# Where the tiles of the normed input begin in SBUF: one place modulo 256 bytes instead of four, with three staging buffers

## The chip, the cores and the metric

The kernel runs on one core of a Trainium2 chip. The time is device microseconds (us) from start to end of one launch. The kernel before took 1615.73 us as the median of three runs (1615.65 to 1615.97).

## What is computed

A trunk of two layers works on 272 tokens (16 learned ones and 256 of the input) of 1024 features, in float32. The first layer computes all 272 tokens; the second needs its outputs for the last 256 alone. Cut to what matters here:

```python
def hybrid_layer(h_res, ...):
    h = rmsnorm(h_res, n_mix_pre)
    proj = jnp.einsum('bld,de->ble', h, w_in)          # 1024 x 17424
    (a_b, a_c, a_x, s_z, s_xbc, s_dt, r_q, r_k, r_v, r_g,
     sb_q, sb_k, sb_v, gate_logits) = jnp.split(proj, IN_SPLITS, axis=-1)
    ...                                                # four token mixers: y_a, y_b, y_c, y_d
    up = jnp.einsum('blnw,nwd->blnd', branches, w_branch)
    merged = jnp.sum(sigmoid(gate_logits) * up, axis=2)
    h_res = h_res + rmsnorm(merged @ w_out, n_mix_post)
    f = rmsnorm(h_res, n_ffn_pre) @ w_ffn_in           # 1024 x 5632
    f = (silu(f_gate) * f_up) @ w_ffn_out              # 2816 x 1024
    return h_res + rmsnorm(f, n_ffn_post)
```

## The kernel before, in words

Features lie on the 128 partitions and tokens on the free axis. The normed input of a sublayer is eight tiles of 128 features (k = 0 to 7). A product is to have float32's precision, so each operand is kept as two addends in float32r: the input tile as `x1` and `x2`, the weight tile as `w1` and `w2`, and every product of a weight tile with an input tile takes three matmuls: (w1, x1), (w2, x1), (w1, x2). The loop is in `mm` (lines 305 to 314, the matmul itself on L313). The weight is the stationary operand (128 columns, 512 bytes of a partition), the input the moving one (256 to 272 columns). While a matmul streams its input, the weight of the next matmul is loaded; the trace shows the loads as a row of their own, PEld. Three matmuls of one k tile are called a triple below.

A job is one tile of 128 output features: eight triples, 24 matmuls into one PSUM bank, and then an evacuation by VectorE. The first layer has 136 such projections of the normed input before the mixers and 44 in the feed-forward part, all 272 columns wide: 180 jobs, 4320 matmuls. The second layer has 116 jobs of 256 columns (2784 matmuls), 44 of 272 (1056), 16 of 258 (384) and 4 of 260 (96). The other matmuls of L313 (2976) have tiles named `hold` as the moving operand: outputs of mixers, of the merge and of the feed-forward part.

`run_jobs` emits the jobs; the order on TensorE is as emitted. The first three jobs after a norm (one in the first norm of all) run side by side, k tile by k tile, so that nine matmuls in a row read one k tile.

Weights come in the order of use (`weights`, line 280): SyncE issues a DMA of 512 KB into a staging buffer `raw` (L287), ScalarE rounds it to `w1` (L298), VectorE subtracts to `w2` (L301). `raw` has four buffers, `w1` and `w2` five each (NW). A staging buffer is free again when L301 has read it. One weight per layer is 16 columns wide (`narrow`, line 316); its staging buffer is read by L328 into `wdt`. A scheduler puts the instructions of ScalarE and VectorE in order; weights have a high priority in it.

The two addends of the input are made in `prenorm` (line 432), by ScalarE (L452) and VectorE (L457), in tiles of 272 floats, eight buffers for each addend. In the second layer a norm starts where the layer needs it, but a matmul may read all 272 columns, or 256 from column 16 on.

Where a tile lies in a partition: the weight tiles take 4096 bytes each and begin, all of them, at 192 modulo 256 in the partition, and so does each k slice of 512 bytes. The tiles of `x1` and `x2` take 272 x 4 = 1088 bytes, which is 4 x 256 + 64, one behind the other. The start of each is therefore 64 bytes further modulo 256 than that of its neighbour: eight tiles fall on four places, two on each. `x1` and `x2` of one k have the same place. Below, the place of a read is the number of bytes modulo 256 from a weight tile's start to the first byte of the input that the matmul reads: 0, 64, 128 or 192.

Of the kernel before, what the change touches and what calls it, by code (L numbers as in the profile page):

```python
# [15 lines left out]
P = 128  # L16
D = 1024
KT = 8
# [8 lines left out]
LATE, LATER = 2, 2  # L27
PS = {"mm": 4, "sc": 1, "ty": 3}
# [9 lines left out]
# token tiles of the sequence mixers and where their columns lie side by side  # L38
# [4 lines left out]
# branches in the order they are merged: index into w_branch  # L43
# [3 lines left out]
# the activation tables that have a function, the one that is loaded by default first  # L47
# [5 lines left out]
def plan():  # L53
    """Weight tiles in the order the kernel uses them: (key, first k tile, k tiles)."""
    out = []

    def proj(l, col):
        out.append((("in", l, col), 0, KT))

    for l in range(DEPTH):  # L60
        def gu(n, m0=0, m1=KT):
            for m in range(m0, m1):
                proj(l, GATE + n * D + m * P)
                out.append((("br", l, n, m), 0, KT))

        def conv(m0, m1):
            for m in range(m0, m1):
                for base in (A_C, A_X, A_B):
                    proj(l, base + m * P)

        for h in range(8):
            for base in (B_K, B_Q, B_V):
                proj(l, base + h * P)
        conv(0, 2)
        proj(l, S_DT)
        for g in range(4):
            for col in (S_XBC + D + g * P, S_XBC + D + 512 + g * P,
                        S_XBC + 2 * g * P, S_XBC + (2 * g + 1) * P,
                        S_Z + 2 * g * P, S_Z + (2 * g + 1) * P):
                proj(l, col)  # L80
            gu(BR_SB, 2 * g, 2 * g + 2)
        for g in range(4):
            for base in (R_K, R_Q, R_V, R_G):
                proj(l, base + 2 * g * P)
                proj(l, base + (2 * g + 1) * P)
        conv(2, 5)
        gu(BR_SSD)
        conv(5, 8)
        gu(BR_RET)
        gu(BR_CONV)  # L90
        for m in range(KT):
            out.append((("out", l, m), 0, KT))
        for j in range(FT):
            out.append((("fi", l, j), 0, KT))
            out.append((("fi", l, FT + j), 0, KT))
        for m in range(KT):
            out.append((("fo", l, m), 0, 8))
            out.append((("fo", l, m), 8, 7))
            out.append((("fo", l, m), 15, 7))
    return out  # L100


def width(key):
    """Columns of a weight tile"""
    return 16 if key[0] == "in" and key[2] == S_DT else P


# per-layer columns of the packed vectors
V_NPRE, V_NPOST, V_FPRE, V_FPOST = 0, 8, 16, 24
V_CA = 32           # 3 x 8  # L110
V_CW = 56           # 4 x 16
V_CB = 120          # 16
V_SN = 136          # 8
V_SD = 144          # 8
V_AL = 152          # 16, the same on every partition
V_DB = 168          # 1, heads on partitions
V_N = 169

# columns of the constants
# [12 lines left out]
def constants():  # L132
    c = np.zeros((P, C_N), np.float32)
    s = np.arange(P)[:, None]
    u = (np.arange(T)[None, :] >= s).astype(np.float32)
    for i, (t0, _) in enumerate(STILE):
        c[:, C_MASK + OFF[i]:C_MASK + OFF[i] + T - t0] = u[:, :T - t0]
    c[:, C_UP:C_UP + T] = u
    c[:, C_MASK:C_MASK + WID] *= 0.25
    rel = np.arange(T)[None, :] - s  # L140
    for h in range(4):
        lg = np.log(1.0 - 2.0 ** (-5.0 - h))
        c[:, C_DEC + h * T:C_DEC + (h + 1) * T] = np.where(
            rel >= 0, np.exp(lg * np.maximum(rel, 0)), 0.0) * (256 ** -0.5)
    inv = (np.float32(10000.0) ** (-np.arange(P, dtype=np.float32) / np.float32(P))).astype(np.float32)
    pos = (PADROWS + np.arange(T)).astype(np.float32)
    ang = (inv[:, None] * pos[None, :]).astype(np.float32).astype(np.float64)
    c[:, C_COS:C_COS + T] = np.cos(ang)
    c[:, C_SIN:C_SIN + T] = np.sin(ang)
    c[:, C_ID:C_ID + P] = np.eye(P)  # L150
    c[:, C_ONE:C_ONE + P] = 1.0
    # lhsT[s, s'] = -1 where s >= s'
    c[:, C_NTRI:C_NTRI + P] = -np.tril(np.ones((P, P)))
    c[:, C_NONE:C_NONE + P] = -1.0
    import ml_dtypes
    b = np.zeros((P, 2 * P), np.float32)
    b[:, :P] = np.eye(P)
    b[:, P:] = np.where(s >= np.arange(P)[None, :], -1e30, 0.0)
    return c, b.astype(ml_dtypes.bfloat16)
# [54 lines left out]
class Trunk:  # L214
    """Features on partitions, tokens on the free axis, throughout.

    The tensor engine takes its work in the order it is emitted here: one tile of 128 output
    features after the other, with the stages of the sequence mixers (generators) between them.
    """
# [16 lines left out]
    # ---- tiles  # L236
# [18 lines left out]
    def table(self, ins):  # L255
        """Functions that need a table keep their order on the scalar engine."""
        if self.last_table is not None:
            self.order(ins, self.last_table)
        self.last_table = ins

    def order(self, ins, before):
        """ins after `before` on the engine of both"""
        self.tc.add_manual_dep(
            ins.ins, before.ins.name,
            mybir.DependencyInfo(mybir.DependencyClass.NoSync, mybir.DependencyReason.DATA),
            reason="order")
# [11 lines left out]
    # ---- weights  # L278
    def weights(self, key):
# [5 lines left out]
        with self.tc.high_priority(offset=1000000):  # L285
            raw = self.t("raw", [P, KT * P], 4)
# [7 lines left out]
            # the first ones in parts, for products to start early  # L294
# [10 lines left out]
    def mm(self, ps, w, k, x1, x2, c0, nk, passes=(0, 1, 2)):  # L305
        """One tile of 128 features against one tile of outputs, in three exact passes."""
# [9 lines left out]
    def narrow(self, ps, key):  # L316
        """Sixteen features, in float32: even and odd k tiles in two halves of the array's columns."""
# [4 lines left out]
        with self.tc.high_priority(offset=1000000):  # L322
            raw = self.t("raw", [P, KT * P], 4)
            nc.sync.dma_start(
                raw[:, :n], self.a["w"][self.woff:self.woff + P * n].rearrange("(p f) -> p f", p=P))
# [10 lines left out]
    def keep_warm(self, n):  # L336
        """Products that nothing reads: the array's clock halves when it idles for a few microseconds."""
# [9 lines left out]
    def run_jobs(self, jobs, first=0, late=0):  # L347
        """jobs: (key, first column, k tiles, operands, evacuation). The `first` jobs run side by
        side, so that each tile of operands is used as soon as it is there. Their outputs, and
        those of `late` more, leave PSUM once the norm's sum is there."""  # L350
# [44 lines left out]
    def two(self, src, c0, scale=1.0):  # L395
        """src (in SBUF or PSUM) as two addends that float32r holds exactly."""
# [10 lines left out]
    def parts(self, src):  # L407
        """src as two addends that float32r holds exactly"""
# [5 lines left out]
    def total(self, out, parts):  # L414
        """Sum over the partitions"""
# [15 lines left out]
    # ---- norms  # L431
    def prenorm(self, c0, vcol, ready=None):
        """The two addends of h * weight; the root mean square is applied where products leave PSUM.
        `ready`: brings a tile of h up to date."""
# [5 lines left out]
        def operands(k):  # L440
            """h's tile k as two addends, and the one after it brought up to date"""
            w = self.v(vcol + k)
            x1 = self.t("x1", [P, T], KT, F32R)
            x2 = self.t("x2", [P, T], KT, F32R)
# [21 lines left out]
            if k == KT - 1 and ready is not None:  # L466
                # prepared before this norm: the tiles that there is room for
# [52 lines left out]
    def postnorm(self, c0):  # L520
        """Gives what norms a tile of the sublayer, and what adds it to h."""
# [17 lines left out]
    # ---- mixers  # L539
    def softplus_part(self, z, tmp, bias=None):  # L540
        """tmp <- ln(1 + exp(-|z + bias|)); the caller adds max(z + bias, 0)."""
# [60 lines left out]
    def silu2(self, out, v):  # L602
        """out <- 2 silu(v), v in SBUF"""
# [4 lines left out]
    def conv4(self, ps, ct, out, cs=0):  # L608
        """Four taps and twice the SiLU of one tile of xbc."""
# [11 lines left out]
    def scaled_silu(self, ps, out):  # L621
        """out <- 2 silu(ps * rstd)"""
# [8 lines left out]
    def ssd_jobs(self, g):  # L631
        """B, C, xs and z of a group; all but z come doubled, z too."""
# [31 lines left out]
    def regions(self):  # L664
        """(index, first token, tokens, first column, where the columns start)"""
# [5 lines left out]
    def both(sc, col, n, step=T):  # L671
        """n columns at col, and n more a step further"""
# [3 lines left out]
    def to_tok(self, srcs):  # L676
        """Transposed token tiles: two full ones in one bank, the last one in another."""
# [20 lines left out]
    def ssd_mix(self):  # L698
        """All groups, one stage after the other."""
# [3 lines left out]
        for g in range(4):  # L703
# [3 lines left out]
            # C B^T under the causal mask; both are doubled, and the mask has a quarter  # L707
# [7 lines left out]
            # xs * dt, tokens on partitions  # L715
# [54 lines left out]
    def ssd_finish(self, out):  # L770
        nc, c0 = self.nc, self.c0
        rr = slice(c0, T)
        # the outputs are doubled by the doubled gate: so is their root mean square
# [126 lines left out]
    def ret_mix(self, h, u):  # L900
# [13 lines left out]
        # values less their mean over the head's width: the outputs then have mean zero  # L914
# [129 lines left out]
    def layer(self, l):  # L1044
# [11 lines left out]
        def late(gen, after=()):  # L1056
            """A generator that starts when others are done"""
# [38 lines left out]
    def run(self, depth):  # L1096
# [19 lines left out]
        # what is loaded after this many tiles of weights  # L1116
# [47 lines left out]
```

## Time and profile before

| | |
|---|---|
| median of three runs | 1615.73 us (1615.65 to 1615.97) |
| the profiled execution, first to last instruction (span) | 1614.1 us |
| median less that span | 1.6 us |
| PE busy | 1599.6 us, 99% of the span |
| matmuls of L313 with the normed input | 8640, 1108.5 us |
| matmuls of L313 with `hold` | 2976, 374.3 us |
| mean granted clock of TensorE | 0.996 |

PE is TensorE's matmuls, PEld its weight loads, DVE is VectorE, ACT ScalarE, POOL GpSimd, SP SyncE; L313 is a line of the kernel. The profile gives the profiled execution by its span alone. Matmuls overlap in their records: one is listed with some 290 ns, but they start every 119 to 126 ns, so the pace is read from starts, or from stretches cut at starts. A row of the windows view gives a stretch (begin and end in us from the span's start), its length, the busy time of PE in it and how many matmuls touch it (those that began before or end behind it too), the granted clock as a share of 2.4 GHz, and the share and rate of the DMA. Its last line sums the stretches. Where the stretches are the triples of one place, each begins at the start of the first matmul of a triple and ends at the start of the next triple.

### The profile page before, as it was taken

Reading aid. Unit: us, or ns where it says so; the run is one execution under the profiler, and the core shown is the slowest. Engines: PE = TensorE matmul, PEld = TensorE weight load, DVE = VectorE, ACT = ScalarE, POOL = GpSimd, SP = SyncE. Lnnn points to the kernel's source line nnn. Section 1 sums busy time; section 2 is a strip of 40 time slices with the busy share of each in tenths; the row PEclk is TensorE's granted clock in tenths of the full one; section 3 lists DMA queues with packets and bytes.
Section 4 is the critical chain, followed back from the end, with each engine's and each line's share of the span. In section 5 each row is a group of like instructions: output and inputs, shape, how many; then the busy total and the mean of one; then the engine's idle time right before and its main releaser. Section 6 shows DMA issues by size and latency. Waiting matters only on the chain.

```text
span 1614.1 us, 31341 instructions
## 1 busy us (share of the span) xinstructions
PE 1599.6 (99%) x12732; PEld 1562.3 (97%) x12732; DVE 1104.0 (68%) x1821; ACT 776.1 (48%) x1142; POOL 301.2 (19%) x284
## 2 busy tenths in 40 slices
PE   9999999999999999999999999999999999999997
PEld 8999999999999999999999999999999999999997
DVE  7557788977866556665465578889878666576643
ACT  5544444445533456444464444444455444564442
POOL 3000003541311112221110000035414111212210
PEclk9999999999999999999999999999999999999999
DMA  7435554434455554555544446544445555545552
GB/s 256 140 120 172 176 178 158 145 118 144 160 179 171 176 177 136 185 176 162 178 141 145 134 146 199 182 171 144 132 144 178 183 188 183 184 158 184 184 181 78
DMA packets 74015, 264.26 MB, mean 164 GB/s; under 512 B 8176, under 2 KB 9744, under 8 KB 73744
## 3 DMA queue, kind: packets, MB, share of 16 engines
q1 hardware_dynamic: 71968, 257.08, 48.5%
q0 software_dynamic: 1216, 4.49, 0.9%
q8 instruction: 100, 1.64, 0.4%
q10 hardware_dynamic: 688, 0.70, 0.1%
q14 instruction: 43, 0.35, 0.1%
HBM read 261.15 MB, written 1.08 MB: 162 GB/s over the span
## 4 chain that ended last, share of the span: by engine, by line
PE 95%; DVE 2%; ACT 1%; POOL 1%; issue 1%; DMA 0%; DVEq 0%; ACTq 0%; POOLq 0%
PE mm L313 87%; PE ty L931 1%; PE ty L847 1%; PE sc L818 1%; PE ty L744 1%; PE sc L908 1%; PE ty L683 1%; DVE w L301 1%; PE sc L834 0%; PE sc L710 0%; PE ty L482 0%; ACT w L298 0%; DVE wide L731 0%; PE ty L690 0%; POOL hold L876 0%
## 5 line engine op out<-in xcount | busy, mean ns | idle before, releaser
L313 PE MATMUL mm<-x,w 128*128 128x272 f32 (+2 forms) x8640 | 1108.5, 288 | 4.2 <-ACT x L452 2.4
L313 PEld LDWEIGHTS mm<-x,w 128*128 128x128 f32 x8640 | 1079.0, 189 | 10.5 <-DVE x L457 3.1
L298 ACT ACTIVATE w<-raw 128x1024 fp32r<-128x1024 f32 (+2 forms) x494 | 512.7, 1040 | 606.1 <-PE mm L313 348.3
L301 DVE TENSOR_TENSOR w<-raw,w 128x1024 fp32r<-128x1024 f32 (+2 forms) x494 | 607.7, 1232 | 261.6 <-ACT w L298 260.6
L313 PE MATMUL mm<-hold,w 128*128 128x272 f32 (+1 forms) x2976 | 374.3, 285 | 0.2 <-DVE hold L403 0.2
L313 PEld LDWEIGHTS mm<-hold,w 128*128 128x128 f32 x2976 | 367.2, 188 | 0.8 <-DVE hold L403 0.7
L1031 POOL TENSOR_TENSOR tmp<-tmp,rstd 128x272 f32<-128x272 f32 (+1 forms) x44 | 61.3, 1394 | 209.6 <-ACT tmp L271 209.6
L735 POOL TENSOR_TENSOR wide<-wide,wide 128x416 f32<-128x416 f32 (+1 forms) x32 | 42.1, 1321 | 243.2 <-ACT wide L271 233.9
L271 ACT ACTIVATE tmp<-tmp 128x272 f32<-128x272 f32 (+2 forms) x176 | 71.3, 412 | 28.3 <-DVE tmp L617 17.5
L1005 POOL TENSOR_TENSOR hold<-hold,tmp 128x272 f32<-128x272 f32 (+1 forms) x48 | 40.0, 834 | 234.3 <-DVE tmp L1003 234.3
L974 POOL TENSOR_TENSOR hold<-hold,rstd 128x272 f32<-128x272 f32 (+1 forms) x16 | 14.0, 876 | 274.2 <-DVE hold L972 249.8
L514 POOL TENSOR_TENSOR tmp<-tmp,tmp 128x272 f32<-128x272 f32 (+1 forms) x24 | 33.0, 1375 | 128.6 <-ACT tmp L507 115.2
L617 DVE SCALAR_TENSOR_TENSOR tmp<-tmp,vec,tmp 128x269 f32<-128x269 f32 (+3 forms) x96 | 47.7, 497 | 2.0
L271 ACT ACTIVATE wide<-wide 128x432 f32<-128x432 f32 (+1 forms) x48 | 26.2, 553 | 33.6 <-DVE wide L731 33.1
L1035 DVE TENSOR_TENSOR tmp<-mm,tmp 128x272 f32<-128x272 f32 (+1 forms) x44 | 19.0, 433 | 29.8 <-POOL tmp L1031 23.6
L1003 DVE SCALAR_TENSOR_TENSOR tmp<-tmp,mm 128x272 f32<-128x272 f32 (+1 forms) x48 | 20.6, 429 | 26.3 <-PE mm L313 25.7
L993 DVE TENSOR_TENSOR tmp<-mm,rstd 128x272 f32<-128x272 f32 (+1 forms) x64 | 27.5, 430 | 15.4 <-PE mm L313 15.0
L399 ACT ACTIVATE hold<-hold 128x272 fp32r<-128x272 f32 (+1 forms) x64 | 25.3, 417 | 20.1 <-DVE hold L978 14.7
L731 DVE TENSOR_SCALAR wide<-acsb,acs_tok 128x16 f32<-128x16 f32 (+3 forms) x96 | 30.4, 366 | 0.0
L606 DVE SCALAR_TENSOR_TENSOR hold<-tmp,tmp 128x272 f32<-128x272 f32 (+1 forms) x64 | 28.6, 457 | 2.2 <-ACT tmp L271 1.1
L533 DVE TENSOR_TENSOR hold<-hold,tmp 128x272 f32<-128x272 f32 (+1 forms) x32 | 13.3, 426 | 21.4 <-ACT tmp L271 21.4
L876 POOL TENSOR_TENSOR hold<-tmp,hold 128x272 f32<-128x272 f32 (+1 forms) x16 | 25.1, 1569 | 0.0
(153 smaller groups left out, 974.9 us busy)
## 6 DMA issues: line engine op xcount, KB each, us to landing
raw<-w SPq DMA_DIRECT2D x456, 512.0 KB, 3.5
raw<-w SPq DMA_DIRECT2D x32, 448.0 KB, 3.3
acsb<-scr POOLq DMA_DIRECT2D x8, 544.0 KB, 5.1
cst<-cst SPq DMA_DIRECT2D x1, 1424.0 KB, 9.7
h<-hT SPq DMA_DIRECT2D x4, 272.0 KB, 4.6
outT<-h SPq DMA_DIRECT2D x2, 256.0 KB, 2.4
outT<-h ACTq DMA_DIRECT2D x2, 256.0 KB, 2.4
vec<-vec ACTq DMA_DIRECT2D x1, 169.0 KB, 4.2
```

The lines of the kernel that those rows point to most:

```text
L271: self.table(self.nc.scalar.activation(out, in_, f, **kw))
L298: ins = nc.scalar.activation(w1[:, c], raw[:, c], AF.Copy)
L301: nc.vector.tensor_tensor(w2[:, c], raw[:, c], w1[:, c].bitcast(F32), ALU.subtract)
L313: self.nc.tensor.matmul(ps[:, c0:T], a, b, start=(k == 0 and p == 0), stop=(k == nk - 1 and p == 2))
L514: nc.gpsimd.tensor_tensor(s[:, r], self.sqsum[:, r], sq[:, r], ALU.add)
L606: self.nc.vector.scalar_tensor_tensor(out, th[:, :v.shape[1]], 1.0, v, ALU.add, ALU.mult)
L617: nc.vector.scalar_tensor_tensor(v[:, s:T], xr[:, cs:T - 3 + i], w(i), v[:, s:T], ALU.mult, ALU.add)
L731: nc.vector.tensor_scalar(m[:, o:o + T - l0], ab[:, j, l0:T], self.acs_tok[:, i, 4 * g + j:4 * g + j + 1], 0.0, ALU.subtract, ALU.min)
L735: nc.gpsimd.tensor_tensor(m[:, c0:OFF[2]], m[:, c0:OFF[2]], cb[:, c0:OFF[2]], ALU.mult)
L993: nc.vector.tensor_tensor(th[:, r], ps[:, r], self.r[:, r], ALU.mult)
L1005: nc.gpsimd.tensor_tensor(self.merged[m][:, r], self.merged[m][:, r], th[:, r], ALU.add)
L1031: nc.gpsimd.tensor_tensor(s[:, r], s[:, r], rs[:, r], ALU.mult)
```

## The change

It does two things. First, the tiles of `x1` and `x2` are 320 floats (1280 bytes, 5 x 256) instead of 272, and the 272 floats that are used begin 48 floats (192 bytes) into the tile, less `self.c0` floats (16 in the second layer, 0 in the first). All tiles then have one place. In the first layer it is 192 for all reads. In the second it is 192 for the reads of 256 columns from column 16 on, 128 for the reads of all 272 columns, and 184 and 180 for those of 258 and 260. Second, the staging buffers `raw` are three instead of four: sixteen input tiles take 16 x 192 = 3072 bytes more, and a staging buffer is 4096. The weight tiles begin at 192 modulo 256 as before. Comments and docstrings are dropped too; the lines of the code change by one or two.

```diff
+XW, XO = 320, 48
 ...
     def weights(self, key):
 ...
-            raw = self.t("raw", [P, KT * P], 4)
+            raw = self.t("raw", [P, KT * P], 3)
 ...
     def narrow(self, ps, key):
 ...
-            raw = self.t("raw", [P, KT * P], 4)
+            raw = self.t("raw", [P, KT * P], 3)
 ...
         def operands(k):
             w = self.v(vcol + k)
-            x1 = self.t("x1", [P, T], KT, F32R)
-            x2 = self.t("x2", [P, T], KT, F32R)
+            x1, x2 = (self.t(n, [P, XW], KT, F32R)[:, XO - self.c0:XO - self.c0 + T] for n in ("x1", "x2"))
```

The order of the instructions on TensorE, GpSimd and SyncE stays as it was. On VectorE and ScalarE the scheduler moves some twenty instructions at the starts of the layers and of the feed-forward parts. VectorE in the first layer, where the narrow weight `wdt` is made from its staging buffer; before:

```order
L823 SCALAR_TENSOR_TENSOR wide_214_1145<-sc_213_1139,wide_214_1145 128x432
L328 TENSOR_TENSOR wdt_276_1495<-raw_275_1493,vec_1_63 128x128
L826 TENSOR_TENSOR wide_216_1151<-wide_214_1145,wide_215_1150 128x432
L796 SCALAR_TENSOR_TENSOR hold_222_1191<-mm_209_1130,rstd_11_91 128x272
L301 TENSOR_TENSOR w2_258_1382<-raw_256_1379,w1_257_1381 128x1024
L801 TENSOR_TENSOR hold_227_1224<-mm_223_1193,rstd_11_91 128x272
L301 TENSOR_TENSOR w2_266_1423<-raw_264_1420,w1_265_1422 128x1024
```

and now:

```order
L824 SCALAR_TENSOR_TENSOR wide_214_1145<-sc_213_1139,wide_214_1145 128x432
L827 TENSOR_TENSOR wide_216_1151<-wide_214_1145,wide_215_1150 128x432
L797 SCALAR_TENSOR_TENSOR hold_222_1191<-mm_209_1130,rstd_11_91 128x272
L303 TENSOR_TENSOR w2_258_1382<-raw_256_1379,w1_257_1381 128x1024
L802 TENSOR_TENSOR hold_227_1224<-mm_223_1193,rstd_11_91 128x272
L303 TENSOR_TENSOR w2_266_1423<-raw_264_1420,w1_265_1422 128x1024
L330 TENSOR_TENSOR wdt_276_1495<-raw_275_1493,vec_1_63 128x128
```

The narrow weight stands two weight tiles later. ScalarE at the start of the second layer's feed-forward part (w is a rounding to `w1`, tmp a SiLU, hold an addend of the result); before:

```order
L298 ACTIVATE w_2991_17343<-raw_17341 128x1024
L298 ACTIVATE w_2996_17378<-raw_17376 128x1024
L271 ACT_TABLE_LOAD
L271 ACTIVATE tmp_17220<-tmp_17220 128x256
L271 ACTIVATE tmp_17229<-tmp_17229 128x256
L298 ACTIVATE w_3002_17414<-raw_17412 128x1024
L399 ACTIVATE hold_17225<-tmp_17220 128x256
```

and now:

```order
L300 ACTIVATE w_2991_17343<-raw_17341 128x1024
L273 ACT_TABLE_LOAD
L273 ACTIVATE tmp_17220<-tmp_17220 128x256
L273 ACTIVATE tmp_17229<-tmp_17229 128x256
L300 ACTIVATE w_2996_17378<-raw_17376 128x1024
L401 ACTIVATE hold_17225<-tmp_17220 128x256
L300 ACTIVATE w_3002_17414<-raw_17412 128x1024
```

One rounding stands behind the table load and two SiLUs instead of ahead of them.

## Rows read from the trace of the kernel before

**Rows 1.** The page: span, and busy time of the engines.

```profile
span 1614.1 us, 31341 instructions
PE 1599.6 (99%) x12732; PEld 1562.3 (97%) x12732; DVE 1104.0 (68%) x1821; ACT 776.1 (48%) x1142; POOL 301.2 (19%) x284
```

**Rows 2.** The page: the chain that ended last, shares of the span.

```profile
PE 95%; DVE 2%; ACT 1%; POOL 1%; issue 1%; DMA 0%; DVEq 0%; ACTq 0%; POOLq 0%
```

**Rows 3.** Groups by form, TensorE: shapes, count | busy us, mean ns | idle before.

```profile
L313 PE MATMUL mm<-x,w 128*128 128x272 f32 x5376 | 712.1, 291 | 3.5 <-DVE x L457 1.7 <-ACT x L452 1.6
L313 PE MATMUL mm<-x,w 128*128 128x256 f32 x2784 | 346.8, 282 | 0.8 <-ACT x L452 0.8
L313 PE MATMUL mm<-hold,w 128*128 128x272 f32 x1488 | 192.4, 288 | 0.1
L313 PE MATMUL mm<-hold,w 128*128 128x256 f32 x1488 | 181.9, 281 | 0.2 <-DVE hold L403 0.2
L313 PE MATMUL mm<-x,w 128*128 128x258 f32 x384 | 48.3, 284 | 0.0
```

**Rows 4.** Windows: first layer's feed-forward projections, 982 matmul starts.

```profile
633.43:757.13 123.70, 123.70 (x983) 1.00 0.55 181
```

**Rows 5.** Windows: the 82 triples at place 192 in that stretch.

```profile
633.43:633.80 0.37, 0.37 (x5) 1.00 0.00 0
...
sum 30.47, PE 30.47; mean PE 0.37
```

**Rows 6.** Windows: the 82 triples at place 128 there.

```profile
sum 31.02, PE 31.02; mean PE 0.38
```

**Rows 7.** Windows: the 82 triples at place 64 there.

```profile
sum 31.42, PE 31.42; mean PE 0.38
```

**Rows 8.** Windows: 81 triples at place 0 there.

```profile
sum 30.78, PE 30.78; mean PE 0.38
```

**Rows 9.** Windows: second layer's feed-forward projections, 256 columns, 81 triples, place 192.

```profile
1425.47:1425.82 0.35, 0.35 (x5) 1.00 1.02 419
...
sum 29.02, PE 29.02; mean PE 0.36
```

**Rows 10.** Windows: 81 triples at place 128 in that stretch of the second layer.

```profile
sum 29.29, PE 29.29; mean PE 0.36
```

**Rows 11.** Windows: 81 triples at place 64 there.

```profile
sum 28.55, PE 28.55; mean PE 0.35
```

**Rows 12.** Windows: 81 triples at place 0 there.

```profile
sum 28.68, PE 28.68; mean PE 0.35
```

**Rows 13.** Windows: seven matmuls in a row at place 192, 272 columns, twice.

```profile
sum 1.74, PE 1.74; mean PE 0.87
```

**Rows 14.** Windows: seven in a row at place 192, 256 columns, twice.

```profile
sum 1.65, PE 1.65; mean PE 0.82
```

**Rows 15.** Windows: first matmuls alone of the 82 triples of rows 5.

```profile
sum 10.38, PE 10.38; mean PE 0.13
```

**Rows 16.** Windows: second matmuls alone of the 82 triples of rows 5.

```profile
sum 9.90, PE 9.90; mean PE 0.12
```

**Rows 17.** The page: the two groups that make weights, and the DMA's landing.

```profile
L298 ACT ACTIVATE w<-raw 128x1024 fp32r<-128x1024 f32 (+2 forms) x494 | 512.7, 1040 | 606.1 <-PE mm L313 348.3
L301 DVE TENSOR_TENSOR w<-raw,w 128x1024 fp32r<-128x1024 f32 (+2 forms) x494 | 607.7, 1232 | 261.6 <-ACT w L298 260.6
...
raw<-w SPq DMA_DIRECT2D x456, 512.0 KB, 3.5
```

**Rows 18.** Waits of the weight loads: total us, times, longest.

```profile
PEld mm L313 <- DVE w L301: 0.6, 2, 0.3
```

**Rows 19.** Timeline at the start: start us, us, engine, line, operands.

```profile
7.56 22.41 SPq L287 DMA_DIRECT2D raw<-w  x6
...
20.12 0.21 DVE L1112 CAST ntri<-cst 128x128 fp32r<-128x128 f32 x1
...
27.30 1.05 ACT L298 ACTIVATE w<-raw 128x1024 fp32r<-128x1024 f32 x1
```

**Rows 20.** Timeline behind the norm of the second layer's feed-forward part.

```profile
1430.91 1.06 ACT L298 ACTIVATE w<-raw 128x1024 fp32r<-128x1024 f32 x1 [0.83 <-DMA raw<-w]
```

## The prediction

> **What bounds the kernel now.** I read the page first, then the chain of waits, the groups by form, the windows, and last the waits. TensorE is busy for 1599.6 of 1614.1 us [rows 1] and 95% of the chain is its own work [rows 2], so the end moves only with the pace of its matmuls or with a new wait on it. The matmuls of L313 hardly wait: 4.3 us before the normed-input forms, a few tenths before `hold` [rows 3], and 0.6 us of waits of their loads for a weight [rows 18]. Both halves of the change are to be judged by this: the first must change the pace, the second must make a weight late.
>
> The pace is read from starts, since the 291 and 282 ns of the groups are overlapping records [rows 3]. In the first layer's feed-forward projections 982 matmuls of 272 columns take 123.70 us at full clock, 126.0 ns each [rows 4]. At 2.4 GHz 272 columns are 113.3 ns, so some 12.7 ns of each are not streaming. The reader should now compare four windows over the same 41 jobs: they differ only in the place of the tile that is read. A triple takes 30.47/82 = 371.6 ns at place 192 [rows 5], 31.02/82 = 378.3 at 128 [rows 6], 31.42/82 = 383.2 at 64 [rows 7] and 30.78/81 = 380.0 at 0 [rows 8]. Per matmul that is 123.9, 126.1, 127.7 and 126.7, on average 126.1. Two k tiles share each place, and I see no other thing that would put k = 1 and 5 together against 2 and 6. So the place matters, by up to 3%.
>
> For 256 columns the ranking differs: 29.02/81 = 358.3 ns at 192 [rows 9], 361.6 at 128 [rows 10], 352.5 at 64 [rows 11], 354.1 at 0 [rows 12]; per matmul 119.4, 120.5, 117.5 and 118.0, on average 118.9. A place is good or bad for a width, not by itself.
>
> The Trainium skill has a rule that speaks against the change. SBUF — State Buffer, section "Who interferes with whom", gives TensorE two independent read ports, one for the moving operand and one for weight loads, and says that it never waits on anyone. By that rule the place of a read could not change the pace, and the sum would be zero from this half. The four windows disagree, 371.6 against 383.2 ns; I let them decide, and keep the rule's result as a rival, as a mechanism of this kernel, below.
>
> **The change, part by part: the place.** After the change every matmul of the first layer with the normed input reads at place 192. A triple at 192 in the trace of before follows one at place 0 and is followed by one at 128, and its three steps are unequal: the first matmul takes 10.38/82 = 126.6 ns [rows 15], the second 9.90/82 = 120.7 [rows 16], and the third, what is left of 371.6, 124.3. The first step seems to carry what its predecessor left. So the tiles alone do not tell what a constant place gives; the nearest rows are the side-by-side jobs at the start of a sublayer, where nine matmuls in a row read one tile. Seven steps inside, twice, at place 192: 1.74 us for 14, 124.3 ns [rows 13]. That agrees with 123.9 of the triples. I take 124.1.
>
> First layer: 180 jobs x 24 = 4320 matmuls, each 126.1 - 124.1 = 2.0 ns shorter: 8.6 us. Bounds: 120.7 each, all on the second step, gives 4320 x 5.4 = 23.3 us; 126.6 each, all on the first step, gives -2.2 us.
>
> Second layer, 256 columns, place 192: 2784 matmuls. The triples say 119.4, worse than the average of 118.9; the same-place runs say 1.65/14 = 117.9 [rows 14], better than it. What comes after the change is like the runs in that the place is constant, and like the triples in the order (w1, w2, w1); I take 118.6, between them. 2784 x 0.3 = 0.8 us gained; bounds 2784 x 1.0 = 2.8 us gained and 2784 x 0.5 = 1.4 us lost.
>
> Second layer, 272 columns, place 128: 1056 matmuls. 126.1 at that place is the average, so zero; with 1 ns either way, 1.1 us. The 480 matmuls of 258 and 260 columns lie at 184 and 180, near 192: zero, 0.5 us either way by the same nanosecond. The 2976 matmuls with `hold` [rows 3] keep a mixture of the four places: zero. ScalarE and VectorE write the same 272 floats into longer tiles: nothing.
>
> **Three staging buffers.** A weight is used up in 24 x 126 = 3.02 us. One staging buffer is held from the issue of its DMA to the end of L301: 3.5 us to landing, 1.04 on ScalarE, 1.23 on VectorE [rows 17] and waits between; without these 5.8 us. Three buffers give 3 x 3.02 = 9.1 us for one round. So 3.3 us stay in a steady stretch, and the waits between are mostly of the harmless kind: 348.3 us of ScalarE's idle time before L298 ended with TensorE, that is, the five pairs `w1`, `w2` were full [rows 17]. These pairs hold up to five weights, 15 us of TensorE's work, and are the cover; with it gone, each late weight would cost what it is late.
>
> Where the cover is thin: at the start, weight 4 now waits for the buffer of the first weight, and its issue moves to the end of the first L301, 7.56 us, where the fifth was issued [rows 19]; the constants' DMA stands behind it in SyncE's queue, then the fifth weight, which goes when weight 2 is done, with the rest of that row. The casts of the constants start only at 20.12, and the next big rounding that needs a later weight at 27.30 [rows 19], far more than a landing after. Behind the norm of the second layer's feed-forward part ScalarE already waits 0.83 us for a DMA with four buffers [rows 20]; with three I expect this to be up to a landing, 3.5 us, at this and two other refills, and at the start. None of it reached TensorE in before: 0.6 us [rows 18]. The narrow weight keeps its buffer two weights longer, since `wdt` moves behind two L301; the next weights are late by at most that, 6 us, against 15 us of stored ones. I cost all this at 0. Bounds: it cannot gain more than the 0.6 us that weights cost now; with no cover at all it loses four landings, 4 x 3.5 = 14.0 us.
>
> **Sum.** 8.6 + 0.8 = 9.4 us off the profiled execution's 1614.1 us: 1604.7. The median of the runs is 1.6 us above that span, so 1606.3.
>
> **The rivals.**
> - No effect of a constant place. The steps of a triple depend on what came before them [rows 15, 16]: the gain at 192 may be paid for by its neighbours, and a steady stream settles at the common 126.1 and 118.9. Against it: the same-place runs at 124.3 [rows 13]. Time: 1615.7, as the skill's rule of independent ports would have it.
> - A larger gain: the stream settles on the second step, 120.7 [rows 16]. For it: that step and the one before it read the same place. Against it: the third step does too and takes 124.3. 23.3 us in the first layer and 2.8 in the second: 1615.7 - 26.1 = 1589.6.
> - Slower by the place: the stream settles on the first step. 4320 x 0.5 = 2.2 us, with 256 columns at the triple's 119.4, 1.4 us, and the 1056 at place 128 one ns worse, 1.1 us: 1620.4. It needs TensorE's stream and loads to keep the phase of a tile's first matmul; rows 13 speak against it.
> - Slower by the staging buffers: at the start and the three refills a landing shows whole on TensorE, 14.0 us, less the gain of 9.4: 1620.3. It decides from the point where the stored pairs run out, when a weight is over 15 us late in a full state; near a norm, with fewer stored, some 5 us. Rows 18 speak against it.
>
> **How the numbers follow.** Forecast 0.62, no effect 0.16, larger gain 0.11, slow phase 0.06, late weights 0.05. What a measurement can tell from no change is 0.2%, 3.2 us, so faster means under 1612.5. The forecast's own bounds are half of the larger gain (122.4 and 117.9 ns: 18.8 us, 1596.9) and a loss of most of it (125.2: 3.9 us, less 1.4 at 256 columns, 1613.2). The range goes to 1596 below and, to take in no effect, to 1616 above; left out are most of the larger gain (0.08) and the slower cases (0.10). Faster: 0.60 of the forecast, the larger gain's 0.11 and 0.02 of late weights that cost less than the gain: 0.73. Within 0.2%: 0.14 of no effect and the forecast's other 0.02: 0.16. Slower: 0.06 of the slow phase, 0.03 of late weights and 0.02 of no effect with small losses: 0.11.
>
> **What would show it.** In the profile after, the windows over the first layer's feed-forward projections: 41 jobs at about 122.1 us against 124.1 for the same 984 starts, and the eight triples of a job equal, near 372 ns. For 256 columns, triples of 353 to 358 ns, all alike. The waits of the weight loads for L301 stay below 2 us. Wrong would be: triples that are all alike at 378 ns; or rows where L313 waits for a weight behind a norm; or a change that comes from elsewhere than L313.

## The result, and the profile after

The changed kernel takes 1595.34 us as the median of four runs (1594.61 to 1597.08), against 1615.76 us of the kernel before beside it (1615.65 to 1615.97). The ratio is 0.9875, 95% interval 0.9861 to 0.9889: 20.4 us less. The forecast was 1606.3 us with a range from 1596 to 1616; the direction was right, the gain was about twice the 9.4 us of the sum, and the time lies 0.7 us under the range.

The head of the page of the kernel after (span, busy time of the engines) answers to [rows 1]:

```profile
span 1593.8 us, 31337 instructions
PE 1578.7 (99%) x12732; PEld 1541.1 (97%) x12732; DVE 1104.1 (69%) x1821; ACT 776.5 (49%) x1142; POOL 299.6 (19%) x284
```

The span is 20.3 us shorter and TensorE's busy time 20.9 us, with the same 12732 matmuls. The other engines are busy as long as before, to 1.6 us. So nothing was waited for less: the matmuls themselves go faster. The groups by form, TensorE, after (the matmul's line is now L315; busy us, mean ns of one record | idle before), answer to [rows 3]:

```profile
L315 PE MATMUL mm<-x,w 128*128 128x272 f32 x5376 | 703.3, 290 | 3.9 <-DVE x L458 1.9 <-ACT x L453 1.6
L315 PE MATMUL mm<-x,w 128*128 128x256 f32 x2784 | 334.1, 278 | 0.7 <-ACT x L453 0.7
L315 PE MATMUL mm<-hold,w 128*128 128x272 f32 x1488 | 192.4, 288 | 0.1
L315 PE MATMUL mm<-hold,w 128*128 128x256 f32 x1488 | 181.8, 281 | 0.2 <-DVE hold L405 0.2
L315 PE MATMUL mm<-x,w 128*128 128x258 f32 x384 | 48.4, 284 | 0.0
```

Against [rows 3] the 272-column form loses 712.1 - 703.3 = 8.8 us and the 256-column form 346.8 - 334.1 = 12.7 us; `hold` and 258 columns stay within 0.1 us. That is 21.5 us, a little more than the 20.3 us of the span, so nothing else is needed for the gain. The reader should see which form gave more: the 256-column one, whose share had been put at 0.8 us.

The windows over the two feed-forward stretches show the pace, one of before first (second layer, not among the rows above; begin and end, length, PE busy and matmuls that touch it, granted clock, DMA):

```profile
1423.14:1540.31 117.17, 117.17 (x986) 1.00 0.60 192
```

The same stretches after, first layer (answers to [rows 4]) and second:

```profile
626.76:748.33 121.57, 121.57 (x986) 1.00 0.58 185
1408.14:1519.86 111.72, 111.72 (x986) 1.00 0.65 201
```

Each holds 984 starts (41 jobs of 24). With 272 columns a matmul now takes 121.57/984 = 123.5 ns against 126.0 [rows 4]; with 256 columns 113.5 against 117.17/984 = 119.1. The triples after, the even k tiles with 272 and then with 256 columns, answer to [rows 5 to 12] (first triple and the sum of 82):

```profile
627.71:628.08 0.37, 0.37 (x5) 1.00 1.12 144
...
sum 30.42, PE 30.42; mean PE 0.37
```

```profile
1409.02:1409.36 0.34, 0.34 (x5) 1.00 0.00 0
...
sum 27.88, PE 27.88; mean PE 0.34
```

30.42/82 = 371.0 ns is what a triple at place 192 took before, 371.6 [rows 5]. 27.88/82 = 340.0 ns is far below every 256-column triple of before, 352.5 to 361.6 [rows 9 to 12]. The place that now holds alone had been the second worst of the four there.

The staging buffers left no mark. The waits of the weight loads for a weight, after, answer to [rows 18]:

```profile
PEld mm L315 <- DVE w L303: 0.7, 2, 0.4
```

0.7 us, as 0.6 before, and the median DMA still lands in 3.5 us.

### The profile page after: what moved, and what is told of

Same layout as the page of the kernel before. It is cut to its first block, busy times and chain, and to the rows that moved or that the text cites. A ratio compares the mean times of both kernels' runs of the same rounds, so it can differ in the third digit from the quotient of the medians.

```text
span 1593.8 us, 31337 instructions
## 1 busy us (share of the span) xinstructions
PE 1578.7 (99%) x12732; PEld 1541.1 (97%) x12732; DVE 1104.1 (69%) x1821; ACT 776.5 (49%) x1142; POOL 299.6 (19%) x284
## 4 chain that ended last, share of the span: by engine, by line
PE 95%; DVE 2%; ACT 1%; POOL 1%; issue 1%; DMA 0%; DVEq 0%; ACTq 0%; POOLq 0%
PE mm L315 86%; PE ty L932 1%; PE ty L848 1%; PE sc L819 1%; PE ty L745 1%; PE sc L909 1%; PE ty L684 1%; DVE w L303 1%; PE sc L835 0%; PE sc L711 0%; PE ty L483 0%; DVE x L458 0%; ACT w L300 0%; DVE wide L732 0%; PE ty L691 0%
## 5 line engine op out<-in xcount | busy, mean ns | idle before, releaser
L315 PE MATMUL mm<-x,w 128*128 128x272 f32 (+2 forms) x8640 | 1087.2, 286 | 4.6 <-ACT x L453 2.4
L315 PEld LDWEIGHTS mm<-x,w 128*128 128x128 f32 x8640 | 1058.8, 189 | 11.0 <-ACT x L453 3.3
L315 PE MATMUL mm<-hold,w 128*128 128x272 f32 (+1 forms) x2976 | 374.2, 285 | 0.3 <-DVE hold L405 0.2
L315 PEld LDWEIGHTS mm<-hold,w 128*128 128x128 f32 x2976 | 366.8, 188 | 0.8 <-DVE hold L405 0.7
```

Source lines behind the costliest of these rows:

```text
L315: self.nc.tensor.matmul(ps[:, c0:T], a, b, start=(k == 0 and p == 0), stop=(k == nk - 1 and p == 2))
```

## The experiments

The expectations name their theories by letters. Theory A: any constant place gives the gain, since no matmul then follows one at another place. Theory B: place 192 is what counts, and another constant place costs what its triples cost in the mixed stream of before. Theory C, in the later runs: 192 is the good place, and its fast pace needs neighbours at 192 too. The rival of C: a read at 192 is fast whatever stands beside it. Apart from these: whether three staging buffers do anything.

**Three staging buffers alone**, on the kernel before:

```diff
-            raw = self.t("raw", [P, KT * P], 4)
+            raw = self.t("raw", [P, KT * P], 3)
```

> The kernel before with three staging buffers and nothing else. Theory (all of the gain is the place): 1615.8 us within 1.5, with waits of L313's loads for a weight below 2 us. Rival (fewer staging buffers change when DMAs land and so what else touches SBUF, and part of the 20.4 us comes from there): 1605 to 1612 us. Second rival (three buffers cost and hide part of the gain of the place): 1618 us or more.

Measured: 1617.09 us, ratio 1.0007 (0.9998 to 1.0017). The 272-column form takes 711.5 us and the 256-column one 346.6, as before; the weight loads wait 0.9 us for weights. The three buffers give nothing and cost nothing that can be told from no change. The whole gain is the place.

**Another constant place**: 64, 128 and 0, with tiles of 1280 bytes and three buffers as after. XO is in floats, 4 bytes each.

```diff
-XW, XO = 320, 48
+XW, XO = 320, 16          # 64; 32: 128; 0: 0
...
-[:, XO - self.c0:XO - self.c0 + T]
+[:, (XO - self.c0) % 64:(XO - self.c0) % 64 + T]
```

> The changed kernel with the tiles at place 64 for the first layer and for the second layer's 256 columns (its 272 columns then read at place 0). Theory A (a constant place is what counts, any of them lets the stream settle): 256 columns settle at 113.3 ns as at place 192, 272 columns near 124, in all 1595 to 1600 us. Theory B (the place 192 is what counts): the triples of the kernel before tell, 127.7 ns at 272 columns and 117.5 at 256; 4320 x 1.6 us/1000 = 6.9 us more and 2784 x 1.4 = 3.9 us less than 1615.8: 1618.8 us.

> The changed kernel at place 128 (the second layer's 272 columns at 64). Theory A: 1595 to 1600 us. Theory B: 126.1 ns at 272 columns and 120.5 at 256, so 1615.8 + 2784 x 1.6 ns = 1620.3 us.

> The changed kernel at place 0 (the second layer's 272 columns at 192, where the first layer's settled at 123.3). Theory A: 1595 to 1600 us. Theory B: 126.7 ns at 272 columns in the first layer, 118.0 at 256, 123.3 for the second layer's 272: 1615.8 + 2.6 - 2.5 - 3.0 = 1612.9 us.

Measured: 1615.27 us, ratio 0.9997 (0.9987 to 1.0006) at 64; 1619.18, 1.0019 (1.0010 to 1.0029) at 128; 1616.40, 1.0004 (0.9994 to 1.0013) at 0. All keep one place for all k tiles, and none gains. Theory A falls. Theory B is right that another place gains nothing of the size, but its prices from the mixed stream are off by 3.5, 1.1 and 3.5 us (1618.8, 1620.3 and 1612.9 were forecast). Windows over the feed-forward stretches of the kernel at place 0, first and second layer:

```profile
632.64:756.17 123.53, 123.53 (x986) 1.00 0.56 182
1422.53:1540.79 118.25, 118.25 (x986) 1.00 0.58 190
```

118.25/984 = 120.2 ns for 256 columns, 6.7 ns more than at 192 after; nothing but the place of the input differs between the two. The table puts the places together; ns per start is the window's length over 984.

| place | 272 columns, ns | 256 columns, ns | time, us |
|---|---|---|---|
| four places mixed (before) | 126.3 | 119.1 | 1615.76 |
| 0 | 125.5 | 120.2 | 1616.40 |
| 64 | 126.9 | 118.0 | 1615.27 |
| 128 | 126.9 | 118.9 | 1619.18 |
| 192 (after) | 123.5 | 113.5 | 1595.34 |
| 176 | 126.9 | 119.5 | 1611.48 |
| 208 | 126.9 | 119.3 | 1617.29 |

(Before, the window with all 984 starts of the first layer is 124.28 us long. The kernel before took 1615.90 us beside the runs at 0, 64 and 128, and 1616.09 beside those at 176 and 208. The columns of ns are of the feed-forward stretches alone.) A place's triple in the mixed stream is no guide for 256 columns: 0 looked good there, 118.0 ns [rows 12], and is the worst of the four alone.

**Sixteen bytes to either side**: is the place a broad valley or a point? 176 by XO = 44; 208 by XO = 20 behind a tile of 128 bytes.

```diff
-XW, XO = 320, 48
+XW, XO = 320, 44          # 176
...
+XW, XO = 320, 20          # 208, with:
+            if not hasattr(self, "gap"):
+                self.gap = self.t("gap", [P, 32], 1)
+                nc.gpsimd.memset(self.gap, 0.0)
```

> The changed kernel with the place 16 bytes lower: 176 (the second layer's 272 columns at 112). If the fast pace belongs to a single place of 16 bytes, 256 columns are back at 118 to 120 ns and the time is 1608 to 1616 us. If the place counts in steps of 64 bytes, 1594 to 1598 us as with the change.

> The changed kernel with the place 16 bytes higher: 208 (a tile of 128 bytes ahead of the input tiles shifts them; the second layer's 272 columns at 144). Single place: 1608 to 1616 us. Steps of 64 bytes: 1594 to 1598 us. A broad optimum around 192 would show as 1594 to 1600 us on this side or the other alone.

Measured: 1611.48 us, ratio 0.9968 (0.9958 to 0.9979) at 176, and 1617.29, 1.0006 (0.9997 to 1.0016) at 208. Sixteen bytes lose a good three quarters of the gain on one side and all of it on the other. What 176 keeps is in jobs of 272 columns outside the feed-forward part (the form takes 705.7 us); its 256 columns gain nothing. Windows of the kernel at 176 over eight jobs of 272 columns each (192 starts), first in the mixers of the first layer, then in its feed-forward part:

```profile
468.67:492.35 23.68, 23.68 (x194) 1.00 0.51 179
637.13:661.47 24.34, 24.34 (x195) 1.00 0.63 207
```

At one and the same place these are 123.3 and 126.8 ns a matmul, both at full clock. By the starts of the jobs, 112 of the 136 ahead of the feed-forward part run at 123 to 124 ns, and so do 34 of the 42 in the second layer (place 112) that do not run side by side. So with 272 columns the fast pace is not bound to place 192; what is lost 16 bytes lower is the pace of the 256 columns and of the feed-forward jobs. The kernel at 208 shows another limit: its four jobs of 260 columns happen to read at 192, and take 119.8 to 120.0 ns a matmul, as at 176 after (120.0 to 120.1; 120.5 before). So 192 is not shown to be good for every width.

**192 and 64 in turn**, even k tiles at 192 and odd ones at 64. Theory C lets a neighbour at 64 spoil the matmuls at 192; its rival adds the prices of the two.

```diff
+    def xo(self, k):
+        return ((XO if k % 2 == 0 else 16) - self.c0) % 64
```

> The changed kernel, but only the even k tiles lie at place 192; the odd ones lie at 64. Theory C (192 is the good place, and its fast pace needs that the reads before it were at 192 too): 192 gives back what the triples of the kernel before show, 256 columns alternate about 119.4 and 117.5 ns, 272 columns 123.9 and 127.7, in all 1612 to 1615 us. Rival (a read at 192 takes 113.3 or 123.4 ns whatever its neighbours are, and the tile's own alignment was the matter): the even triples keep 340 and 370 ns, half of the gain stays, 1603 to 1606 us.

Measured: 1608.35 us, ratio 0.9952 (0.9937 to 0.9967), between the forecasts of C and of its rival. Triples of 256 columns in the feed-forward stretch, first those at 192, then those at 64 (first triple and the sum of 82):

```profile
1418.75:1419.09 0.35, 0.35 (x5) 1.00 0.00 0
...
sum 28.37, PE 28.37; mean PE 0.35
```

```profile
sum 29.03, PE 29.03; mean PE 0.35
```

28.37/82 = 346.0 ns at 192 between tiles at 64, 354.0 at 64. At 192 alone it is 340.0, and 358.3 in the mixed stream [rows 9], between places 0 and 128. So one and the same read at 192 costs 340, 346 or 358 ns by what stands beside it. The rival of C is wrong in this, but C went too far too: it expected 358 again, and half a stream at 192 keeps a good third of the gain.

**Is it the relation to the weights, or the address?** A gap of 64 bytes ahead of the staging buffers moves weights and input together: the weights begin at 0 modulo 256 instead of 192, the place stays 192.

```diff
+        if not hasattr(self, "gap"):
+            self.gap = self.t("gap", [P, 16], 1)
+            nc.gpsimd.memset(self.gap, 0.0)
```

> The changed kernel with a tile of 64 bytes ahead of the staging buffers: weight tiles at 0 instead of 192 modulo 256, input at 192 instead of 128, still at place 192 to each other. If the relation between the two reads counts, 1594 to 1598 us, 256 columns at 113.3 ns. If the address modulo 256 of either read alone counts, 1608 to 1618 us.

Measured: 1595.66 us, ratio 0.9873 (0.9859 to 0.9888), as after. The distance between the two reads decides, not where either of them lies, as far as one step of 64 bytes can show. Places 176 and 208 also take the input off a multiple of 64 bytes; no run moves both operands by 16, so for those two the distance and the alignment of the input are not told apart.

**The other input, `hold`, at 192 too.** The change left these 2976 matmuls at a mixture. Longer tiles need room, which four weight pairs and nine `tmp` buffers make; the second kernel does that alone.

```diff
-NTMP, NHOLD, NW = 10, 51, 5
+NTMP, NHOLD, NW = 9, 51, 4
...
-        return self.t("hold", [P, T], NHOLD, dt)
+        return self.t("hold", [P, XW], NHOLD, dt)[:, HO - self.c0:HO - self.c0 + T]   # HO = 32
```

> The changed kernel with the 51 tiles called hold at place 192 as well (1280 bytes each; the room comes from four instead of five weight pairs and nine instead of ten tmp tiles). Theory C: the 1488 matmuls of 272 columns with hold go from 125.7 to 123.4 ns, the 1488 of 256 columns from 118.4 to 114, 3.4 + 6.5 us less than the changed kernel: 1585 to 1587 us. Rival (fewer weight pairs let L313 wait): over 1595 us, with waits of the weight loads for w.

> The changed kernel with four instead of five weight pairs and nine instead of ten tmp tiles, hold as in the change: what the kernel with hold at 192 gave up for its room. Theory (the 11 us between that kernel and the change come from the place of hold): as the change, 1595 us within 1.5. Rival (fewer buffers help by themselves): 1585 to 1590 us. It costs if the loads of L313 wait for weights: over 1597 us.

Measured: 1584.19 us (1583.82 to 1591.23, three of the four runs within 0.7 us), ratio 0.9813 (0.9793 to 0.9833), with `hold` at 192; 1596.92, 0.9882 (0.9866 to 0.9899), with fewer buffers alone. Groups by form, TensorE, of the kernel with `hold` at 192:

```profile
L315 PE MATMUL mm<-x,w 128*128 128x256 f32 x2784 | 333.4, 278 | 0.7 <-ACT x L453 0.7
L315 PE MATMUL mm<-hold,w 128*128 128x272 f32 x1488 | 189.3, 287 | 0.1
L315 PE MATMUL mm<-hold,w 128*128 128x256 f32 x1488 | 174.6, 276 | 0.3 <-DVE hold L405 0.3
```

and of the kernel with fewer buffers alone:

```profile
L315 PE MATMUL mm<-x,w 128*128 128x256 f32 x2784 | 335.9, 279 | 0.7 <-ACT x L453 0.7
L315 PE MATMUL mm<-hold,w 128*128 128x272 f32 x1488 | 192.7, 289 | 0.1
L315 PE MATMUL mm<-hold,w 128*128 128x256 f32 x1488 | 181.4, 281 | 0.2 <-DVE hold L405 0.2
```

The same place works on another tensor, and again more at 256 columns (6.8 us) than at 272 (3.4 us); the input's 256 columns give 2.5 us more. These 2.5 us are the two paces told of below: by the starts, 10 of its 112 jobs run at the slower one with `hold` at 192 and 34 with fewer buffers alone (17 after), and 24 jobs x 24 x 4.4 ns are 2.5 us. The forecasts were missed by little: 0.8 us under the 1585 to 1587 with `hold` at 192, and 0.4 us over the 1595 within 1.5 of the fewer buffers, which the 17 slower jobs more than after explain. The version with `hold` at 192 is the fastest, some 32 us under before and 11 under after.

**The kernel after once more**, for the two paces told of below.

> The changed kernel once more, for the number of 256-column jobs that run at 118 instead of 113 ns in another execution (17 of 112 in the first profile, 1595.6 us). If these jobs make the spread of its runs (1594.61 to 1597.08 us), each is worth 24 x 4.5 ns = 0.11 us: a profiled execution of 1594.6 has 8 of them or so, one of 1597 some 30.

Measured: 1595.22 us (1594.99 to 1595.76), ratio 0.9871 (0.9856 to 0.9886), with 18 jobs of 112 at the slower pace, 17 in the first profile. The profiled executions took 1595.76 and 1595.60 us, too alike to show that the count of such jobs sets the time; between kernels it shows, as told of the fewer buffers. All 17 slower jobs of the first profile are among the 18, so which job is slow follows the program more than the execution.

## Why the prediction was right or wrong

**What bounds it, and where the change acts: right.** TensorE's pace set the end, the place set the pace, and the change comes from L313 alone. The rule that the prediction weighed, in the Trainium skill's page SBUF — State Buffer, section "Who interferes with whom", has the two read ports of TensorE independent; the zero that was drawn from it is not what the runs show, with 113.5 against 120.2 ns at two places (192 and 0) of kernels that are otherwise alike, and 20.4 us in the time.

**First layer, 4320 matmuls, 126.1 to 124.1 ns, 8.6 us: right, a little small.** The window gives 121.57 us where 122.1 was forecast, 123.5 ns. At 2.5 ns each (126.0 less 123.5) this is 10.8 us. The 272-column form as a whole shows 8.8 us, because 1056 of its matmuls lie at place 128, where a constant stream takes 126.6 ns by the starts of its jobs where 126.1 was forecast, some 0.5 us more in all, and because the beginning of this execution ran at a lower clock. The window of 10 to 20 us, after:

```profile
10.00:20.00 10.00, 9.92 (x38) 0.51 0.57 213
```

The granted clock is 0.51 there, near the 1.2 GHz level; before, the same window had 0.66, and the 120th matmul of the loop in `mm` starts 1.3 us later after than before. The repeat of the kernel after had 0.72 and a 272-column form of 702.3 us: this differs by execution and is no effect of the change.

**Second layer, 256 columns, place 192: the step that failed.** It said: "The triples say 119.4, worse than the average of 118.9; the same-place runs say 1.65/14 = 117.9 [rows 14], better than it ... I take 118.6, between them", with at most 2.8 us to gain. It is 12.7 us, 4.6 ns each. Both rows were read rightly, and both misled. The triples of [rows 9] read at 192 between tiles at places 0 and 128, and the turn of 192 and 64 shows that the neighbours count, 346.0 against 358.3 ns. And the side-by-side runs of [rows 14], in which the place is constant, show the slower of two paces that the same reads can have. Windows of after at place 192 with 256 columns, two stretches of 20 starts, each inside one job, and two of five starts in side-by-side runs:

```profile
1049.89:1052.25 2.36, 2.36 (x22) 1.00 0.60 223
1222.81:1225.08 2.27, 2.27 (x22) 1.00 0.46 143
1399.46:1400.05 0.59, 0.59 (x7) 1.00 0.00 0
1404.49:1405.06 0.57, 0.57 (x7) 1.00 0.00 0
```

In each pair the matmuls take 117.8 and then 113.4 ns (2.356 and 2.267 us, 0.589 and 0.567 us by the unrounded starts), at full clock, with the same shapes and places. A job keeps the pace in which it settles: the first stays at 117 to 120 ns to its end, the second goes 120, 117, 116, 114, 113 and stays. In this profile 95 of the 112 jobs run at 113 and 17 at 118, and these 17 stand behind transposes and other work of the mixers or behind `hold`, never behind a job of the normed input. The 117.9 of [rows 14] agrees with the slower pace, and the prediction took it for the price of the place. So its bound was no bound: it lacked the case that a long constant stream reaches a pace that no row of before shows.

**272 columns at place 128, 258 and 260 columns, `hold`: right at zero**, with 0.5 us lost at the first. (The reads of 260 columns lie at 176, not at 180: they begin 12 columns, 48 bytes, behind the 128 of the 272. Their form takes 12.2 us before and after.) That `hold` was left at a mixture was worth 10 us to the kernel of the experiment above.

**Three staging buffers: right at zero.** 1.0007 alone, and waits of 0.7 to 0.9 us for weights. The stored pairs cover the thin places, as said.

**The rivals.** "No effect" and "slow phase" fall with place 192; "late weights" falls with the buffers alone. "Larger gain", 1589.6 us, is the nearest in time but not in place: it had 23.3 us in the first layer by a pace of 120.7 ns, which no job of 272 columns keeps, and 2.8 us at 256 columns.

**The signs named.** Triples of 272 columns all equal near 372 ns: 371.0 and 369.0 (even and odd k). Triples of 256 columns at 353 to 358, all alike: alike, but 340.0. This one sign was the failed step's.

## What to carry to other kernels

Where a matmul stream fills TensorE, compute for both operands the address modulo 256 and try the constant distances on the chip: here one of the six constant distances tried gives 1.3% and the others 0.3% or less, and 16 bytes to either side of the good one most or all of the gain is gone. Try each width that the kernel uses, and look at more than one stretch. Do not price a place from a stream in which places alternate, or from a few matmuls behind an interruption: the steady pace of a long constant stream can lie below every row of the old trace, so such a row bounds the gain on neither side. Apply what is found to every moving operand; here the second tensor gave 12.7 us more than its control.

## What the hardware showed that was not expected

- The distance between moving operand and weight changes a float32r matmul's pace at equal shapes: in the feed-forward stretches 256 columns take 113.5 ns at 192 and 118.0 to 120.2 at the five other distances, 272 columns 123.5 and 125.5 to 126.9. Moving both by 64 bytes changes nothing (1595.66 us).
- One kernel has two steady paces for the same shapes and places, 113.4 and 117.8 ns, and keeps one through a job. At place 64 eight jobs of 112 reach 113 ns too; with 272 columns at 192, 175 of 176 jobs are at 123, and at 176 the same shapes run at 123.3 and 126.8.
- By the Trainium skill, page TensorE: Matmul & The Clock Gate, section "Back-to-back issue gap", the gap of an isolated matmul is N/2.4 + 2.5 ns, and in a stream of weight loads and matmuls both set the spacing. The formula would be an estimated 109.2 ns for 256 columns and 115.8 for 272. No stretch measured here reaches it; the best are 340.0/3 = 113.3 and 369.0/3 = 123.0, in the triples of after.

Open: why 192, why two paces, and what sends a job into one of them. The profile shows starts and ends of matmuls and weight loads, not what happens between the reads, and no run separates the reads of the moving operand from the loads of the weights.
